# A fused two-layer backbone on one core: how the first stage normalises, turns and empties its token tiles

## The chip, the cores and the metric

The kernel runs on one core of a Trainium2 chip. Its engines are named as the profile names them: PE is TensorE (matrix products, and transposes as products with an identity matrix), DVE is VectorE, ACT is ScalarE, POOL is GpSimd, SP is SyncE, which here only issues DMA transfers. The metric is the time of one execution on the device in microseconds (us); the trace comes from one profiled execution.

## The reference

Two consecutive layers work on 512 latent tokens and 256 context tokens of 1024 features. The first layer mixes tokens by gated linear attention and softmax attention, the second by a gated recurrence, and each ends with a SwiGLU block. Every sub-layer begins with an RMS norm and a shift and scale computed from a conditioning vector. Only the first of these matters here:

```python
def _rms(x, gain, eps=1e-6):
    y = xf * lax.rsqrt(jnp.mean(xf * xf, axis=-1, keepdims=True) + eps)
    ...
m_lat = jnp.split((sc @ mod_w[l] + mod_b[l])[:, None, :], 6, axis=-1)
h_lat = _modulate(_rms(x_lat, norm_pre_mix[l]), m_lat[0], m_lat[1])   # h * (1 + scale) + shift
... h @ w_in ...
```

## The kernel before

Tokens are handled in six tiles of 128: tiles 4 and 5 hold the context, 0 to 3 the latents, and the first stage takes them in the order 4, 5, 0, 1, 2, 3. A tile arrives with tokens on the 128 partitions. Products need the features there, so a tile is first normalised, then turned by TensorE in eight 128 x 128 transposes into an accumulator of 1024 columns (`mm_tile`, of which there are two), and then copied into `xT`. Matrix products use a number split in a high and a low part, and three products for one.

`turn(t)` does this for one tile. `sumsq` has ScalarE square the tile and sum each row, then read out the sum (`ss`). `rstd` (lines 684 and 686) divides by the length and adds the epsilon on VectorE (`ms`), and raises to the power -1/2 on POOL (`rs`). VectorE scales the tile in place (line 1945). After the transposes ScalarE empties the first half of the accumulator and VectorE the second (line 1952). `issue_after` only puts VectorE's scaling of a tile behind an earlier instruction in VectorE's queue: here behind VectorE's copy of the tile two places earlier.

`warm(n)` issues n products of the identity with itself into an unused accumulator `idle`. Each is two matmul rows in the trace. `sums(qd, ks)` multiplies the conditioning vectors with one quarter of the modulation weights `mraw`, `cols(qd)` turns the result into columns (`modrows`, `modT`, `modcol`, `aff`), and `apply` computes scale and shift of two feature blocks of `xT` twice: on ScalarE rounded into the high part (line 2005), and on VectorE in full (line 2006), from which the high part is subtracted (line 2007). `z(t0, qd)` multiplies with a quarter of the first projection (`nat`), whose raw numbers `zraw` are split by `weights(qd)`: the high part on ScalarE (line 792), the low part `wL` on POOL (line 793). The loads of `mraw` and `zraw` are issued by SP, 16 pairs and four pieces; nine buffers hold the pairs, so the tenth pair and later ones wait until `sums` has used an earlier one.

The order on each engine is set by a scheduler that models the time of each instruction. Between `self.pinned = True` and `False` TensorE's instructions stay in the order in which they are written; the other queues are ordered by the model, so an edit can move instructions that it does not name. `self.behind()` puts what follows behind the instructions in `self.latest` in their queues.

Of the kernel before, what the change touches and what calls it, by code (L numbers as in the profile page):

```python
# [8 lines left out]
F32 = mybir.dt.float32  # L9
F32R = mybir.dt.float32r  # L10
BF16 = mybir.dt.bfloat16
U8 = mybir.dt.uint8
AF = mybir.ActivationFunctionType
ALU = mybir.AluOpType
# [3 lines left out]
P = 128  # L18
D = 1024
KD = D // P  # L20
# [7 lines left out]
EPS = 1e-6  # L28
# [288 lines left out]
class Net:  # L317
# [371 lines left out]
    def sumsq(self, src, junk=None, ss=None):  # L689
        if junk is None:  # L690
            junk = self.wp.tile([P, D], BF16, tag="mraw", bufs=2, name="junk")[:, : src.shape[-1]]
        if ss is None:
            ss = self.sm.tile([P, 1], F32, tag="ss", name="ss")
        self.squared = self.nc.scalar.activation(junk, src, AF.Square, accum_out=ss)
        return ss

    def pre_norm(self, pool, t, xt, A, B, h, xn):

        nc = self.nc
        r = 0 if t < LT else 1  # L700
        forms = isinstance(h, Forms)
        if forms:
            xn = pool.tile([P, D], F32, tag="xn", bufs=2, name=f"xn{t}")
        rs = self.rstd(self.sumsq(xt, xn if forms else None), D)
        yield
        if not forms:
            self.mark = nc.vector.tensor_scalar(xn, xt, rs, None, op0=ALU.mult)
            self.pair.append(xn)
            if len(self.pair) == 2:
                self.turns.append(self.pair_turn(pool, t - 1, self.pair, A, B, h))  # L710
                self.pair = []
            return
        self.mark = nc.vector.tensor_scalar(xn, xt, rs, None, op0=ALU.mult)

        def turn():
            for hf in range(2):
                pt = self.tr_tile(f"hT{t}{hf}")
                f = h.at(hf, t)
                for kk in range(4):
                    k = hf * 4 + kk  # L720
                    self.tr(pt[:, kk * P : (kk + 1) * P], xn[:, k * P : (k + 1) * P], self.ident)
                for kk in range(4):
                    k = hf * 4 + kk
                    src = pt[:, kk * P : (kk + 1) * P]
                    nc.scalar.activation(f[:, kk, :], src, AF.Identity, bias=B[:, r, k : k + 1], scale=A[:, r, k : k + 1])
                h.put(hf, t)

        self.turns.append(turn)
# [375 lines left out]
    def even_mixer(self, h, mix, z):  # L1104
# [141 lines left out]

        self.pinned = True
        run("qk0 e m qk0 e e v0 qk0 e e m qk0 e e m v0 e e m m q v0 m m v0 m m kv q m q m q m m m m m m m m m m qk1 kv m")
        tp.release()
        gp = self.open_pool("gla")  # L1250
        run("c0 l0 kv m c0 kv c0 v1 qk1 c0 p p qk1 c0 l0 p qk1 l0 c0 g0 qk1 l0 p c1 p v1 l0 p v1 l0 c1 p v1 l0 c1 l1 g1 g0 c1 g0 r0 c1 l1 r0 g0 l1")
        self.tc.keep_in_program_order(nc.scalar.preload_act_table_set("exp_and_others"))
        run("r0 c1 g1 x l1 x g1 l1 x x l1 x l1 x")
        gp.release()
        mg.__exit__(None, None, None)
# [652 lines left out]
    def run(self):  # L1908
        nc, I, out = self.nc, self.I, self.out
# [13 lines left out]
        order = (4, 5, 0, 1, 2, 3)  # L1923
# [4 lines left out]
        with self.pool("pre0") as pp:  # L1928
            xT = pp.tile([P, KD, NT], F32, name="xT")
# [7 lines left out]
            emptied = []  # L1937

            def turn(t):
                xt = xts.pop(t)  # L1940
                ss = self.sumsq(xt)
                with ExitStack() as behind:
                    if len(emptied) > 1:
                        behind.enter_context(self.tc.issue_after(emptied[-2][1].ins))
                    nc.vector.tensor_scalar(xt, xt, self.rstd(ss, D), None, op0=ALU.mult)
                pt = self.mm_tile(f"xT{t}")
                for k in range(KD):
                    self.tr(pt[:, k * P : (k + 1) * P], xt[:, k * P : (k + 1) * P], self.ident)
                for hf in range(2):
                    dst = xT[:, hf * 4 : hf * 4 + 4, t * P : (t + 1) * P]  # L1950
                    src = pt[:, 512 * hf : 512 * hf + 512].rearrange("p (k i) -> p k i", k=4)
                    self.latest = [*self.latest[-1:], (nc.vector.tensor_copy if hf else nc.scalar.copy)(dst, src)]
                emptied.append(self.latest)

            self.mod_tiles(0, (0, 1))
            A = self.cst.tile([P, 2, 8], F32, name="aff01")
# [4 lines left out]
            def loads(qd):  # L1961
                for k in range(0, KD, 2):
                    u = pp.tile([P, 2, 2, 256], F32, tag="mraw", bufs=9, name=f"mraw00{qd}{k}")
                    for kk in range(2):
                        nc.sync.dma_start(
                            out=u[:, kk],
                            in_=I["mod_w"][0, (k + kk) * P : (k + kk + 1) * P, 0:2048].rearrange("p (m f) -> p m f", m=2)[
                                :, :, 256 * qd : 256 * qd + 256
                            ],
                        )  # L1970
                    us[qd, k] = u
                src = w[256 * qd : 256 * qd + 256, 1536 : 1536 + 288].rearrange("(k p) m -> p k m", p=P)
                zu.append(self.fetched(src, 2, 288, pp.tile([P, 576], F32, tag="zraw", bufs=4, name="zraw")))

            def sums(qd, ks):
                if ks[0] == 0:
                    accs[qd] = (self.sc_tile("mod_acc", qd) if qd < 2 else self.tr_tile("mod_acc"))[:, :P]
                for k in ks:
                    for j in range(4):
                        self.mm(  # L1980
                            accs[qd][32 * j : 32 * j + 32, :],
                            self.scT[:, k, :],
                            us[qd, k // 2 * 2][:, k % 2, j // 2, (j % 2) * P : (j % 2) * P + P],
                            start=(k == 0),
                            stop=(k == KD - 1),
                            tile_position=(0, 32 * j),
                        )
                if ks[-1] == KD - 1:
                    accs[qd] = self.mod_cols(0, accs[qd], P, [(m, r, 2 * qd, 2 * m, r, 2) for m in range(2) for r in range(2)])
# [9 lines left out]
            def apply(qd, r, t0, n):  # L1999
                tok = slice(t0 * P, (t0 + n) * P)  # L2000
                for k in range(2 * qd, 2 * qd + 2):
                    H, L = h.hl(k, tok)
                    a, b = A[:, r, k : k + 1], B[:, r, k : k + 1]
                    f = pp.tile([P, SEQ], F32, tag="xa", bufs=4, name="xa")[:, : n * P]
                    cast = nc.scalar.activation(H, xT[:, k, tok], AF.Identity, bias=b, scale=a)  # L2005
                    nc.vector.tensor_scalar(f, xT[:, k, tok], a, b, op0=ALU.mult, op1=ALU.add)
                    self.mark = nc.vector.tensor_tensor(L, f, H.bitcast(F32), op=ALU.subtract)
                    self.latest = cast, self.mark

            def weights(qd):  # L2010
                with self.behind():
                    zu[qd] = zu[qd](vector=nc.gpsimd)
# [20 lines left out]
            fetch(*order)  # L2033
            for qd in range(4):
                loads(qd)
            for t, n in zip(order[:-1], (1, 2, 2, 3, 3)):
                turn(t)
                self.warm(n)
            sums(0, lo)
            turn(order[-1])  # L2040
            self.warm(3)
            sums(0, hi)
            weights(0)
            self.warm(2)
            cols(0)
            self.warm(5)
            apply(0, 1, 4, 2)
            apply(0, 0, 0, 4)
            for qd in range(1, 4):
                z(4, qd - 1)  # L2050
                sums(qd, lo)
                z(0, qd - 1, (0,))
                sums(qd, hi)
                weights(qd)
                z(0, qd - 1, (1,))
                cols(qd)
                z(2, qd - 1)
                apply(qd, 1, 4, 2)
                apply(qd, 0, 0, 4)
# [217 lines left out]
```

## Time and profile before

| What | Value |
|---|---|
| Device time, median of 3 runs | 1681.68 us (1681.31 to 1683.89) |
| Profiled execution, its own time | 1683.77 us |
| Its span, first to last instruction | 1681.9 us |
| TensorE busy | 1647.9 us, 98% |
| VectorE busy | 1311.9 us, 78% |
| ScalarE busy | 915.6 us, 54% |
| POOL busy | 127.4 us, 8% |
| Mean granted TensorE clock | 0.998 of full speed |

A row of the timeline gives start, duration, engine, line, operation, output and inputs, shapes, and how many instructions were merged; in brackets stands how long the engine was idle before it and what released it. A row of the windows gives, for a stretch of time, the busy time of PE, PEld (the weight loads beside the products), DVE, ACT and POOL with their instruction counts, then the granted clock, the share of the DMA engines and their GB/s. A row of groups gives a line, its forms and count, the busy time and the mean duration in ns.

### The profile page before, as it was taken

How to read it: one execution, taken by the hardware profiler on the slowest of the kernel's cores; microseconds unless marked ns; L12 is line 12 of the kernel's file. 1: busy time of each engine (PE TensorE's matmuls, PEld its weight loads, DVE VectorE, ACT ScalarE, POOL GpSimd, SP SyncE). 2: the span in 40 equal slices, each digit the busy share in tenths (PEclk: the TensorE clock that was granted, in tenths of full speed). 3: DMA queues.
4: the chain of work that ended last, by engine and by line, in shares of the span. 5: the costliest groups of instructions: out<-in, count | busy, mean ns of one | idle time of the engine just before them, and what ended most of it. 6: DMA issues, size and time to landing. Idle time of an engine off the chain costs nothing.

```text
span 1681.9 us, 32570 instructions
## 1 busy us (share of the span) xinstructions
PE 1647.9 (98%) x13425; PEld 1484.2 (88%) x13425; DVE 1311.9 (78%) x2106; ACT 915.6 (54%) x1554; POOL 127.4 (8%) x133
## 2 busy tenths in 40 slices
PE   8999998999999999999999999999999999999998
PEld 7899987888999999998887788888888899999886
DVE  4889768876898988768668648788775589988887
ACT  4645557846544443445447536566564565555564
POOL 2004200001000000002101000000000100000310
PEclk9999999999999999999999999999999999999999
DMA  9651002164253446249515542121125333433973
GB/s 332 190 155 42 2 27 101 52 199 156 85 150 101 141 144 189 79 134 223 100 57 210 191 132 64 52 60 43 52 62 152 125 103 114 123 101 101 221 167 138
DMA packets 184736, 204.79 MB, mean 122 GB/s; under 512 B 7142, under 2 KB 141836, under 8 KB 184588
## 3 DMA queue, kind: packets, MB, share of 16 engines
q1 hardware_dynamic: 173996, 181.98, 34.6%
q0 software_dynamic: 9024, 17.30, 5.9%
q10 hardware_dynamic: 1568, 3.43, 0.6%
q8 instruction: 105, 1.72, 0.4%
q14 instruction: 43, 0.35, 0.1%
HBM read 193.23 MB, written 9.46 MB: 121 GB/s over the span
## 4 chain that ended last, share of the span: by engine, by line
PE 83%; DVE 9%; DMA 3%; ACT 3%; issue 2%; POOL 0%; DVEq 0%; SPq 0%; ACTq 0%; POOLq 0%
PE nat L355 12%; PE a L355 10%; PE ff L355 8%; PE E L355 7%; PE x L355 7%; PE oproj L355 6%; PE o L355 5%; PE b L355 3%; PE D L355 3%; PE fq L355 3%; PE gqk L355 2%; PE pearly L355 2%; PE q L355 2%; PE S L355 2%; PE poh L355 1%
## 5 line engine op out<-in xcount | busy, mean ns | idle before, releaser
L355 PE MATMUL nat<-wH,x 128*128 128x256 f32 (+2 forms) x968 | 226.7, 322 | 0.8 <-ACT x L2005 0.2
L849 ACT CAST wH<-raw 128x1024 fp32r<-128x1024 f32 x120 | 124.8, 1050 | 105.1 <-DVE raw L874 40.1
L355 PEld LDWEIGHTS nat<-wH,x 128*128 128x128 f32 x968 | 162.0, 190 | 19.1 <-ACT natq L1185 1.7
L850 DVE TENSOR_TENSOR wL<-raw,wH 128x1024 fp32r<-128x1024 f32 x120 | 145.6, 1220 | 25.1 <-ACT wH L849 24.5
L355 PE MATMUL nat<-wL,x 128*128 128x256 f32 (+2 forms) x484 | 153.5, 317 | 1.8 <-DVE wL L793 1.8
L793 DVE TENSOR_TENSOR wL<-raw,wH 128x1024 fp32r<-128x1024 f32 x79 | 95.7, 1221 | 48.5 <-ACT wH L792 47.7
L355 PE MATMUL ff<-x,wH 128*128 128x512 f32 (+1 forms) x512 | 127.7, 340 | 0.0
L686 POOL TENSOR_TENSOR rs<-ms,neghalf 128x1 f32<-128x1 f32 (+2 forms) x62 | 62.9, 1018 | 793.9 <-DVE ms L684 793.8
L792 ACT CAST wH<-raw 128x1024 fp32r<-128x1024 f32 x79 | 82.2, 1050 | 66.9 <-PE ff L355 20.0
L355 PE MATMUL oproj<-wH,x 128*128 128x512 f32 x320 | 102.2, 394 | 0.4 <-ACT x L1319 0.4
L355 PEld LDWEIGHTS nat<-wL,x 128*128 128x128 f32 x484 | 92.1, 190 | 7.8 <-DVE wL L793 2.6
L615 DVE SCALAR_TENSOR_TENSOR macc<-mraw,scT,macc 128x1024 f32<-128x1024 f32 x70 | 88.0, 1279 | 11.5 <-DMA mraw<-in_mod_w_dram 11.3
L355 PEld LDWEIGHTS ff<-x,wH 128*128 128x128 f32 x512 | 87.3, 190 | 10.0
L355 PE MATMUL x<-wH,two 128*128 128x512 f32 x280 | 90.5, 392 | 0.8 <-DVE y L1840 0.7
L1762 POOL DMA_DIRECT2D t<-in_ffn_w_down_dram x36 | 41.8, 1199 | 642.5 <-DVE t L1801 335.0
L1001 ACT COPY qkh<-arr 128x512 f32<-128x512 f32 x112 | 70.0, 641 | 36.4 <-DVE arr L1006 32.2
L355 PE MATMUL ff<-x,wL 128*128 128x256 f32 (+1 forms) x256 | 86.2, 337 | 0.0
L874 DVE TENSOR_TENSOR raw<-raw 128x512 f32<-128x512 f32 x120 | 82.7, 689 | 2.8
L1006 DVE TENSOR_TENSOR arr<-arr,f 128x512 f32<-128x512 f32 x112 | 74.1, 686 | 1.9 <-ACT qkh L1001 0.3
L355 PE MATMUL a<-T,wH 128*128 128x384 f32 (+1 forms) x320 | 70.6, 309 | 2.0 <-ACT qb L912 1.2
L355 PEld LDWEIGHTS oproj<-wH,x 128*128 128x128 f32 x320 | 59.9, 188 | 13.1 <-ACT x L1319 1.0
L355 PE MATMUL a<-x,dH 128*128 128x384 f32 (+1 forms) x320 | 70.4, 309 | 1.0 <-ACT go L922 0.6
(423 smaller groups left out, 4558.7 us busy)
## 6 DMA issues: line engine op xcount, KB each, us to landing
mraw<-in_mod_w_dram SPq DMA_DIRECT2D x80, 512.0 KB, 4.2
raw<-in_ffn_w_gate_dram SPq DMA_DIRECT2D x44, 512.0 KB, 3.9
raw<-in_ffn_w_up_dram SPq DMA_DIRECT2D x44, 512.0 KB, 4.8
raw<-in_odd_w_in_dram SPq DMA_DIRECT2D x40, 512.0 KB, 3.8
t<-in_ffn_w_down_dram POOLq DMA_DIRECT2D x30, 512.0 KB, 8.5
raw<-in_ffn_w_down_dram SPq DMA_DIRECT2D x28, 512.0 KB, 7.7
mraw<-in_mod_w_dram SPq DMA_DIRECT2D x32, 256.0 KB, 6.2
raw<-in_even_w_in_dram SPq DMA_DIRECT2D x16, 512.0 KB, 5.9
```

The source lines that it names most:

```text
L355: return self.pin(self.nc.tensor.matmul(*a, **k))
L615: nc.vector.scalar_tensor_tensor(a, u, w, a, op0=ALU.mult, op1=ALU.add)
L686: nc.gpsimd.tensor_tensor(rs, ms, self.neghalf.to_broadcast([P, w]), op=ALU.pow)
L792: self.casts = self.casts[-1:] + [nc.scalar.copy(H[:, :m], raw[:, :m])]
L793: vector.tensor_tensor(L[:, :m], raw[:, :m], H[:, :m].bitcast(F32), op=ALU.subtract)
L849: self.nc.scalar.copy(H, f)
L850: self.nc.vector.tensor_tensor(L, f, H.bitcast(F32), op=ALU.subtract)
L874: add = lambda o, x, y: nc.vector.tensor_tensor(o, x, y, op=ALU.add)
L1001: nc.scalar.copy(qkv[:, :, :, half, :], dst)
L1006: nc.vector.tensor_tensor(dst, dst, tb, op=ALU.mult)
L1762: add = lambda o, src: self.pin(nc.gpsimd.dma_start(out=o, in_=src, accum_op=ALU.add))
```

## The change

Five edits, all in the first stage. `mean_rstd` replaces `sumsq` and `rstd` for these six tiles: ScalarE's square gets the factor 1/32, so that its sum is the mean already, and POOL adds the epsilon and takes the power; VectorE has no part. An accumulator is emptied by one engine in one copy of 1024 columns: VectorE takes the first, second and fifth tile in order (4, 5 and 2), ScalarE the others (0, 1 and 3). The scaling of the third tile is no longer put behind a copy; that of the fourth stands behind the first tile's copy, those of the fifth and sixth behind the second's. Behind tile 5's transposes 18 identity products follow in place of 2. `self.latest` is set by hand for `weights(0)`, which it puts behind the last two copies. The new name in `apply` changes no instruction.

```diff
+    def mean_rstd(self, src):
+        nc = self.nc
+        junk = self.wp.tile([P, D], BF16, tag="mraw", bufs=2, name="junk")
+        ms = self.sm.tile([P, 1], F32, tag="ss", name="ss")
+        self.squared = nc.scalar.activation(junk, src, AF.Square, scale=1.0 / 32, accum_out=ms)
+        rs = self.sm.tile([P, 1], F32, tag="rs1", name="rs")
+        nc.gpsimd.tensor_scalar(ms, ms, EPS, None, op0=ALU.add)
+        nc.gpsimd.tensor_tensor(rs, ms, self.neghalf, op=ALU.pow)
+        return rs
...
             def turn(t):
                 xt = xts.pop(t)
-                ss = self.sumsq(xt)
+                rs = self.mean_rstd(xt)
                 with ExitStack() as behind:
-                    if len(emptied) > 1:
-                        behind.enter_context(self.tc.issue_after(emptied[-2][1].ins))
-                    nc.vector.tensor_scalar(xt, xt, self.rstd(ss, D), None, op0=ALU.mult)
+                    if len(emptied) > 2:
+                        behind.enter_context(self.tc.issue_after(emptied[min(len(emptied) - 3, 1)].ins))
+                    nc.vector.tensor_scalar(xt, xt, rs, None, op0=ALU.mult)
...
-                for hf in range(2):
-                    dst = xT[:, hf * 4 : hf * 4 + 4, t * P : (t + 1) * P]
-                    src = pt[:, 512 * hf : 512 * hf + 512].rearrange("p (k i) -> p k i", k=4)
-                    self.latest = [*self.latest[-1:], (nc.vector.tensor_copy if hf else nc.scalar.copy)(dst, src)]
-                emptied.append(self.latest)
+                copy = nc.vector.tensor_copy if len(emptied) in (0, 1, 4) else nc.scalar.copy
+                emptied.append(copy(xT[:, :, t * P : (t + 1) * P], pt.rearrange("p (k i) -> p k i", k=KD)))
...
-            for t, n in zip(order[:-1], (1, 2, 2, 3, 3)):
+            for t, n in zip(order[:-1], (1, 18, 2, 3, 3)):
                 turn(t)
                 self.warm(n)
             sums(0, lo)
             turn(order[-1])
             self.warm(3)
             sums(0, hi)
+            self.latest = emptied[5], emptied[4]
             weights(0)
```

VectorE's queue at the program's start, before. `xt4` is tile 4 as loaded, `xT4` its accumulator, `xT_122` the turned tokens; numbers behind an underscore tell buffers apart.

```order
L684 TENSOR_SCALAR ms_197<-ss_195 128x1
L684 TENSOR_SCALAR ms_217<-ss_215 128x1
L1945 TENSOR_SCALAR xt4_126<-xt4_126,rs_199 128x1024
L1945 TENSOR_SCALAR xt5_128<-xt5_128,rs_219 128x1024
L419 COPY col_103<-pt_rows_109 128x128
L1952 COPY xT_122<-xT4_202 128x4x128
L684 TENSOR_SCALAR ms_238<-ss_236 128x1
L1945 TENSOR_SCALAR xt0_130<-xt0_130,rs_240 128x1024
L1952 COPY xT_122<-xT5_222 128x4x128
L684 TENSOR_SCALAR ms_259<-ss_257 128x1
L1945 TENSOR_SCALAR xt1_132<-xt1_132,rs_261 128x1024
```

The same queue now.

```order
L1956 TENSOR_SCALAR xt4_126<-xt4_126,rs_197 128x1024
L1956 TENSOR_SCALAR xt5_128<-xt5_128,rs_215 128x1024
L1956 TENSOR_SCALAR xt0_130<-xt0_130,rs_250 128x1024
L419 COPY col_103<-pt_rows_109 128x128
L1961 COPY xT_122<-xT4_201 128x8x128
L1961 COPY xT_122<-xT5_219 128x8x128
L1956 TENSOR_SCALAR xt1_132<-xt1_132,rs_269 128x1024
L1956 TENSOR_SCALAR xt2_134<-xt2_134,rs_289 128x1024
L1956 TENSOR_SCALAR xt3_136<-xt3_136,rs_326 128x1024
L1961 COPY xT_122<-xT2_293 128x8x128
```

The scaling of tile 0 now stands ahead of the copies of tiles 4 and 5, the scalings of tiles 1 to 3 right behind those, and the six means are gone.

TensorE's queue at the same place, as a difference. `idle` rows are the identity products, `xT` rows the turns of tiles 4, 5, 0 and 1.

```order
-L358 MATMUL xT_222<-ident,xt_128 128x128 x8
+L358 MATMUL xT_219<-ident,xt_128 128x128 x8
+L355 MATMUL idle<-ident 128x128 x18
+L358 MATMUL xT_254<-ident,xt_130 128x128 x8
 L355 MATMUL idle<-ident 128x128 x2
-L358 MATMUL xT_243<-ident,xt_130 128x128 x8
-L355 MATMUL idle<-ident 128x128 x2
-L358 MATMUL xT_264<-ident,xt_132 128x128 x8
+L358 MATMUL xT_273<-ident,xt_132 128x128 x8
```

The turn of tile 0 (`xt_130`) now follows 18 identity products; everything behind it keeps its order.

POOL's queue now. Before, six powers (line 686) stood here alone.

```order
L704 TENSOR_SCALAR ss_195<-ss_195 128x1
L704 TENSOR_SCALAR ss_213<-ss_213 128x1
L705 TENSOR_TENSOR rs_197<-ss_195,neghalf_99 128x1
L705 TENSOR_TENSOR rs_215<-ss_213,neghalf_99 128x1
L704 TENSOR_SCALAR ss_248<-ss_248 128x1
L705 TENSOR_TENSOR rs_250<-ss_248,neghalf_99 128x1
```

The model puts the addition of tile 5 ahead of the power of tile 4. On ScalarE three whole copies (tiles 0, 1 and 3) stand where six halves stood, and on SP the last piece of `zraw` moves from behind the last quarter's `mraw` loads to behind the first two of these eight.

More of the change, by code (lines that the diff above doesn't have):

```diff
@@ L2003, in apply @@
                     a, b = A[:, r, k : k + 1], B[:, r, k : k + 1]
+                    x = xT[:, k, tok]
                     f = pp.tile([P, SEQ], F32, tag="xa", bufs=4, name="xa")[:, : n * P]
-                    cast = nc.scalar.activation(H, xT[:, k, tok], AF.Identity, bias=b, scale=a)
-                    nc.vector.tensor_scalar(f, xT[:, k, tok], a, b, op0=ALU.mult, op1=ALU.add)
+                    cast = nc.scalar.activation(H, x, AF.Identity, bias=b, scale=a)
+                    nc.vector.tensor_scalar(f, x, a, b, op0=ALU.mult, op1=ALU.add)
                     self.mark = nc.vector.tensor_tensor(L, f, H.bitcast(F32), op=ALU.subtract)
```

## The prediction

> **What bounds it now.** The page's engine table comes first: TensorE is busy 98% of the span, so a microsecond taken out of its queue anywhere is worth about a microsecond, and one taken from another engine is worth what TensorE waits for it.
>
> ```profile
> PE 1647.9 (98%) x13425; PEld 1484.2 (88%) x13425; DVE 1311.9 (78%) x2106; ACT 915.6 (54%) x1554; POOL 127.4 (8%) x133
> ```
>
> The change lies in the first 28 us, so I then read the timeline there. I call a 128-token tile by its number: 4 and 5 are context, 0 to 3 latent, taken in the order 4, 5, 0, 1, 2, 3.
>
> ```profile
> 1.64 5.99 PE L355 MATMUL idle<-ident 128*128 128x128 f32 x36 [1.64 <-POOL ident masks.py:199]
> ...
> 6.79 0.19 ACT L694 ACTIVATION_READ_ACCUMULATOR junk<-xt 128x1 f32 x1
> ...
> 7.10 0.75 DVE L1945 TENSOR_SCALAR xt<-xt,rs 128x1024 f32<-128x1024 f32 x1
> 7.25 1.02 POOL L686 TENSOR_TENSOR rs<-ms,neghalf 128x1 f32<-128x1 f32 x1 [0.72 <-DVE ms L684]
> ...
> 7.95 1.05 PE L358 MATMUL xT<-ident,xt 128*128 128x128 f32 x8
> ...
> 8.30 0.75 DVE L1945 TENSOR_SCALAR xt<-xt,rs 128x1024 f32<-128x1024 f32 x1 [0.45 <-POOL rs L686]
> ...
> 9.11 1.09 PE L358 MATMUL xT<-ident,xt 128*128 128x128 f32 x8
> ...
> 12.39 1.05 ACT L1952 COPY xT<-xT 128x512 f32<-128x512 f32 x2
> ...
> 12.98 0.69 DVE L1952 COPY xT<-xT 128x512 f32<-128x512 f32 x1 [3.73 <-ACT xT L1952]
> ...
> 13.81 0.55 POOL L686 TENSOR_TENSOR rs<-ms,neghalf 128x1 f32<-128x1 f32 x1 [5.55 <-DVE ms L684]
> 14.40 0.75 DVE L1945 TENSOR_SCALAR xt<-xt,rs 128x1024 f32<-128x1024 f32 x1 [0.66 <-POOL rs L686]
> ...
> 15.30 1.78 PE L358 MATMUL xT<-ident,xt 128*128 128x128 f32 x8 [4.65 <-DVE xt L1945]
> ```
>
> TensorE turns tiles 4 and 5 by 10.2 and then waits 4.65 us for tile 0 to be scaled. VectorE had not begun that: its next instruction was its half of emptying tile 4's accumulator, which waited 3.73 us for ScalarE's half, and ScalarE had all six squares ahead of it until 12.39. The windows show a second price.
>
> ```profile
> 8.62:10.65 2.03, 2.03 (x18) 1.76 (x16) 0.63 (x2) 1.88 (x3) 0.00 (x0) 1.00 1.01 394
> 10.65:15.30 4.65, 0.00 (x1) 0.03 (x1) 1.65 (x4) 2.62 (x7) 0.55 (x1) 1.00 1.10 350
> ...
> 15.45:18.87 3.42, 3.42 (x18) 3.42 (x18) 1.87 (x5) 0.59 (x1) 0.79 (x2) 0.51 1.10 358
> ```
>
> The column ahead of the last two is the granted clock. After the empty 4.65 us it is 0.51 for 3.42 us and then full again; the last but one is the share of the DMA engines, at 1.0 and over. The chain of waits gives what TensorE does from there to tile 3, the last tile turned.
>
> ```profile
> 15.30 1.78 PE xT L358 x8
> 17.08 0.85 PE idle L355 x4
> 17.93 1.41 PE xT L358 x8
> 19.34 0.67 PE idle L355 x6
> 20.01 0.10 issue
> ...
> 21.85 1.01 PE mod_acc L355 x32
> 22.86 1.02 PE xT L358 x8
> ```
>
> So 7.56 us from tile 0 to tile 3, and from tile 3 the rest of the stage follows TensorE's own queue until the first product of the projection.
>
> ```profile
> 16.48 0.75 DVE L1945 TENSOR_SCALAR xt<-xt,rs 128x1024 f32<-128x1024 f32 x1 [0.66 <-POOL rs L686]
> ...
> 17.11 0.59 ACT L1952 COPY xT<-xT 128x512 f32<-128x512 f32 x1 [3.67 <-PE xT L358]
> ...
> 17.73 0.69 DVE L1952 COPY xT<-xT 128x512 f32<-128x512 f32 x1 [0.50 <-ACT xT L1952]
> ...
> 19.21 0.75 DVE L1945 TENSOR_SCALAR xt<-xt,rs 128x1024 f32<-128x1024 f32 x1 [0.73 <-POOL rs L686]
> ...
> 25.15 1.41 POOL L793 TENSOR_TENSOR wL<-zraw,wH 128x576 fp32r<-128x576 f32 x1 [3.71 <-ACT wH L792]
> ...
> 27.65 0.40 PE L355 MATMUL nat<-wH,x 128*128 128x288 f32 x1 [0.23 <-ACT x L2005]
> ...
> 27.89 0.29 PE L355 MATMUL nat<-wL,x 128*128 128x288 f32 x1
> ```
>
> **Norms on POOL.** Six VectorE instructions at line 684 go, and six additions on POOL come. No row shows a POOL addition of one column; the nearest are these, with two copies of the new width further down the list.
>
> ```profile
> masks.py:199 POOL TENSOR_SCALAR_AFFINE_SELECT ident<-ident 128x128 f32<-128x128 f32 x1 | 0.3, 288 | 0.0
> ...
> L386 POOL MEMSET neghalf<- 128x1 f32 x1 | 0.1, 97 | 0.0
> ...
> L764 DVE TENSOR_TENSOR pn<-oproj,gv 128x1024 f32<-128x1024 f32 x10 | 12.2, 1220 | 16.3 <-ACT junk L694 16.1
> ...
> L694 ACT ACTIVATE junk<-oproj 128x1024 bf16<-128x1024 f32 x10 | 10.2, 1019 | 25.4 <-PE oproj L355 25.4
> ```
>
> I take 0.29 us, since the select is also a one-input operation with constants, with 0.10 (the memset) and 0.55 (the power) as ends. POOL's queue now holds addition 4, addition 5, power 4, power 5, so power 4 still waits for the second square, read out at 6.98. POOL starts about 0.09 after what it waits for (the second mean ended at 7.16, the power began at 7.25). Addition 5 runs 7.07 to 7.36 and power 4 ends at 7.91. Scaling 4 starts 0.03 later (8.27 to 8.30 above), runs 7.94 to 8.69, and the turn of tile 4 starts 0.10 after that (7.85 to 7.95), at 8.79 where it was at 7.95. Power 5 overlaps scaling 4. In the row at 7.25 such a power took 1.02 and ended 0.42 after the scaling beside it; so it ends at 9.11, and scaling 5 at 9.89. The turn of tile 4, 1.02 by the chain's row, ends at 9.81, its one identity product (two matmul rows of 0.112) at 10.03, so tile 5 is turned from 10.03 to 11.05.
>
> The Trainium skill, "SBUF — State Buffer", section "Who interferes with whom", has it that whichever of the two issues first keeps the shared ports for its whole instruction and the other blocks. The row at 7.25 agrees, the scaling having begun first; here power 5 would issue at 7.91, ahead of the scaling at 7.94, and by that rule scaling 4 would lose 0.55, the turn of tile 5 would end at 11.60, and the gain below would be 1.38 in place of 1.93.
>
> **Scalings ahead of copies, one engine for an accumulator.** VectorE no longer meets the wait of 3.73 us: scaling 0 stands ahead of the copies. Its addition and power need 0.84 of POOL after 9.11, or end 0.42 past scaling 5 at 10.3 if they are held, so it ends by about 11.1, and the copies of tiles 4 and 5 follow whole, 1.22 each by the row with a 1024-wide accumulator operand, after one of 128 columns: by 12.6 and 13.8. Scalings 1 to 3 of 0.75 are done by 16.1. ScalarE's whole copies take 1.02 against 0.59 for a half. Both lie beside TensorE's identity products. What is late next is neither of them.
>
> **Sixteen more identity products.** TensorE must finish 18 of them, 36 rows at 0.112 us (0.67 for six in the chain), 4.02 us, before it may turn tile 0: 11.05 to 15.07. Tile 0 and its accumulator are ready at about 12.6, so the products are the bound, and the turn begins only 0.23 earlier than 15.30. But TensorE is not empty for 4.65 us any more; I expect no stretch at 0.5. Then four turns' worth of queue costs, at full speed, 3 turns of 1.02, four identity rows 0.45, twice six at 0.67 and the sums 1.01: 5.86 in place of 7.56. Tile 1 wants its scaling (by 14.6) and tile 5's accumulator (13.8) at 16.5; tile 2 wants ScalarE's copy of tile 0 (about 17.2) at 18.2. All come in time. Tile 3 starts at 15.07 + 5.86 = 20.93 instead of 22.86.
>
> **Sum.** 0.23 from the earlier turn and 1.70 from the clock: 1.93 us against the profiled execution's 1683.77 (span 1681.9 and 1.87 around it), which would be 1681.84. The square's new factor and the renamed operand of the affine step issue the same instructions as before, and POOL's next work is not due until 25.15: nothing for these. Behind tile 3 nothing changes but that ScalarE's last copy is 0.43 longer, so the low weights come 0.43 later against tile 3; they ended at 26.56 and were wanted at 27.89, which covers it, and without that cover it would cost what exceeds 1.33. The profiled execution is 2.1 above the median of 1681.68, and I can't say how the unprofiled runs fell on the clock. Had the clock stayed full there, tile 0 would have been turned 0.7 sooner, but VectorE would then bind: it is free for the copy of tile 0 only when scaling 1 ends at 17.23, and copy, mean and power ahead of scaling 2 take 1.48 (17.73 to 19.21): scaling 2 done at 19.46, turn at 19.56 for 20.11, only 0.55 better. So the gain against such runs is 1.38. I take the middle, 1.65: 1681.68 - 1.65 = 1680.0.
>
> Ends: with the addition at 0.10 and power 5 not held, tile 5's turn ends at 10.86 and the gain is 2.12. With 0.55 and scaling 4 held, it ends at 11.86: 1.12, less 0.55 for an undisturbed clock, 0.57.
>
> **The loads.** The third and fourth quarter's loads on SP's queue wait for buffers that the sums free, and one load of the projection's weights is moved ahead of six of the last quarter's. Both matter only if the DMA engines, full at this time, come late.
>
> ```profile
> L355 PE MATMUL mod_acc<-mraw,scT x256: 272/273/297, 21.8 to 48.6; 128*32 128x128 f32 x128
> L1965 SPq DMA_DIRECT2D mraw<-in_mod_w_dram x32: 367/368/1092, 5.8 to 33.9; - x32
> ...
> DMA to landing us min/median/max: 4.6/6.2/7.4
> ```
>
> The last load is issued at 33.9 and lands by 41.3; its product is at 48.6, about 47 after the change. A load of 128 x 2 x 288 numbers, 0.295 MB, moved ahead at 350 GB/s (last column of the windows) costs it 0.84. That leaves some 5 us, so I count no loss.
>
> **Rivals.** First, POOL costs more than I think, as at the high end: gain 0.6 to 1.1, some 1680.8. For it, that powers of one column take longer elsewhere:
>
> ```profile
> 366.35 1.53 POOL L686 TENSOR_TENSOR rs<-ms,neghalf 128x1 f32<-128x1 f32 x1 [63.58 <-DVE ms L684]
> ```
>
> Second, the slow side: POOL's queue, addition 5 and both powers at 1.53 each. Power 4 then ends at 10.13, scaling 4 at 10.9, power 5 at 11.66, scaling 5 at 12.44, and tile 5's turn at 13.6. TensorE would stand empty from 7.8 to 11, lose the clock as it did after 10.65 (another 1.70), and the 36 rows would end at 17.6 or later: 0.6 + 1.7 slower, 1684.0. The change loses time once tile 5's turn ends after 12.98 (22.86 less 5.86 and 4.02). Against it: the power at 13.81 took 0.55, and nothing on VectorE but two scalings overlaps these.
>
> Third, the clock falls all the same between the turn of tile 5 and tile 0. The identity rows would run at 0.213 (0.85 for four in the chain) from about 12 to 15.45: 9 rows before, 16 in the slow stretch, 11 after, ending at 16.7, tile 3 at 22.5, gain 0.3: 1681.4. Against it: 8.62 to 10.65 is mostly turns, and the clock stayed 1.00 through it. The Trainium skill, "TensorE: Matmul & The Clock Gate", "Part 4: PE-mode transpose", says that transposes do not count as busy time in the same way; no row here shows that they fail to hold the clock, and by that rule this third case is what would happen.
>
> Fourth, the change does nothing: TensorE's earlier start is spent waiting for `mraw`, 1681.7. Against it the 5 us above.
>
> **Numbers.** Forecast 0.68; POOL dearer 0.14; slow side 0.08; clock falls 0.05; transfers 0.05. The range holds the ends (1679.6 to 1681.1), the third and fourth case, and something for the shown runs' spread of 1681.31 to 1683.89: 1678.4 to 1682.2. A difference of 0.2%, 3.4 us, is about what a measurement of this kernel can tell. No case gains that much; only the best end, 2.12, with a median 1.2 lower by chance gives it: 0.08 for faster. Slower by as much needs the slow case well beyond its 2.3: 0.05. The rest, 0.87, is within it.
>
> **What would show it.** Right: tile 4 turned near 8.8; tile 0 near 15.1, following the identity products with no gap; granted clock 1.00 from 10 to 20; tile 3 near 20.9, the first projection product near 25.7; no wait of TensorE on `mraw` before 50. Wrong: an addition far from 0.3, an empty TensorE ahead of tile 4 of over 3 us, a slow clock within 9 to 21, or a TensorE wait on VectorE's copies.

## The result and the profile after

| What | Before | After |
|---|---|---|
| Device time, median of 20 runs each | 1681.74 us (1679.95 to 1684.77) | 1679.93 us (1678.06 to 1681.13) |
| Ratio after/before | | 0.9985, 95% interval 0.9978 to 0.9991 |
| Profiled execution, its own time | 1683.77 us | 1680.16 us |
| Its span | 1681.9 us | 1678.4 us |
| First product of the projection | 27.65 us | 25.22 us |

The whole run is 0.15% shorter by the ratio, 1.5 to 3.7 us by its interval. The middle lies under the 0.2% (3.4 us) that was taken for what a measurement of this kernel can tell, the upper end a little above. The stage itself can be read far more finely, because both traces begin alike. The timeline after, the same stretch as was shown of before:

```profile
7.35 1.39 POOL L705 TENSOR_TENSOR rs<-ss,neghalf 128x1 f32<-128x1 f32 x2
...
7.95 1.58 DVE L1956 TENSOR_SCALAR xt<-xt,rs 128x1024 f32<-128x1024 f32 x2 [7.95 <-POOL rs L705]
...
8.76 1.09 PE L358 MATMUL xT<-ident,xt 128*128 128x128 f32 x8 [0.59 <-DVE xt L1956]
8.83 0.78 POOL L704 TENSOR_SCALAR ss<-ss 128x1 f32<-128x1 f32 x1
...
9.91 1.04 PE L358 MATMUL xT<-ident,xt 128*128 128x128 f32 x8
...
10.29 0.75 DVE L1956 TENSOR_SCALAR xt<-xt,rs 128x1024 f32<-128x1024 f32 x1 [0.76 <-POOL rs L705]
...
10.79 4.18 PE L355 MATMUL idle<-ident 128*128 128x128 f32 x36
...
11.16 2.35 DVE L1961 COPY xT<-xT 128x1024 f32<-128x1024 f32 x2
...
11.86 0.22 POOL L704 TENSOR_SCALAR ss<-ss 128x1 f32<-128x1 f32 x1
...
14.81 1.04 PE L358 MATMUL xT<-ident,xt 128*128 128x128 f32 x8
...
20.32 1.09 PE L358 MATMUL xT<-ident,xt 128*128 128x128 f32 x8
...
23.11 1.41 POOL L804 TENSOR_TENSOR wL<-zraw,wH 128x576 fp32r<-128x576 f32 x1 [8.90 <-ACT wH L803]
...
24.27 0.26 DVE L2003 SCALAR_TENSOR_TENSOR aff<-modcol,col 128x4 f32<-128x4 f32 x1
...
25.22 0.40 PE L355 MATMUL nat<-wH,x 128*128 128x288 f32 x1 [0.26 <-ACT x L2014]
```

Tile 4 is turned at 8.76 and tile 5 at 9.91, 0.8 later than before; the 36 identity rows follow at once and tile 0 behind them at 14.81 with no idle time in brackets. VectorE no longer waits for ScalarE: scaling 0 begins at 10.29, the two whole copies at 11.16. The chain of waits of the same run gives TensorE's queue (start, duration, what):

```profile
10.95 4.02 PE idle L355 x36
14.97 0.87 PE xT L358 x8
15.84 0.45 PE idle L355 x4
16.29 0.87 PE xT L358 x8
...
19.38 1.01 PE mod_acc L355 x32
20.39 1.02 PE xT L358 x8
```

And the windows (busy times of PE, PEld, DVE, ACT, POOL, then the granted clock, DMA share and GB/s) have no slow stretch, where before 15.45 to 18.87 had 0.51:

```profile
10.65:14.81 4.16, 4.16 (x40) 4.16 (x39) 4.16 (x7) 1.70 (x5) 3.14 (x6) 1.00 1.10 350
14.81:20.32 5.51, 5.51 (x75) 5.19 (x73) 1.91 (x3) 2.03 (x2) 0.00 (x0) 1.00 1.10 356
```

TensorE's waits of the first 75 us are these alone (us in total, times, longest); none is for `mraw` and none for a copy:

```profile
PE idle L355 <- POOL ident masks.py:199: 1.6, 1, 1.6
PE xT L358 <- DVE xt L1956: 0.6, 1, 0.6
PE nat L355 <- ACT x L2014: 0.3, 1, 0.3
```

So the stage gains 2.43 us at the first product. The spans differ by 3.5. Set beside each other instruction by instruction, the changed kernel leads by 2.4 up to 160 us, by 1.0 from 208 to 600, and by about 2.0 from 680. The fall stands at two places in its profile, 161.78 and 206.27 us, where TensorE had been idle for 0.56 and 0.46 us and nothing is shown that it waited for. Near 1373 us the lead jumps by about 2, where the profiled run of before had this row among TensorE's waits from 1360 to 1430:

```profile
PE a L355 <- ACT qb L912: 1.2, 1, 1.2
```

With two smaller waits beside it, it lost 2.1 us. A second profiled execution of the kernel before, told below, has no TensorE wait in that stretch, and one of the experiments has them again, so this part comes and goes by itself.

### The profile page after: what moved, and what is told of

The parts are those of the page before. It is cut to its first block, busy times and chain, and to the rows that moved or that the text cites. A ratio compares the mean times of both kernels' runs of the same rounds, so it can differ in the third digit from the quotient of the medians.

```text
span 1678.4 us, 32622 instructions
## 1 busy us (share of the span) xinstructions
PE 1649.9 (98%) x13457; PEld 1486.4 (89%) x13457; DVE 1311.4 (78%) x2097; ACT 915.6 (55%) x1551; POOL 131.5 (8%) x139
## 4 chain that ended last, share of the span: by engine, by line
PE 83%; DVE 8%; ACT 3%; DMA 3%; issue 2%; POOL 0%; DVEq 0%; SPq 0%; ACTq 0%; POOLq 0%
PE nat L355 12%; PE a L355 10%; PE ff L355 8%; PE E L355 7%; PE oproj L355 6%; PE x L355 6%; PE o L355 4%; PE D L355 4%; PE b L355 4%; PE fq L355 3%; PE gqk L355 2%; PE pearly L355 2%; PE q L355 2%; PE S L355 2%; PE poh L355 1%
## 5 line engine op out<-in xcount | busy, mean ns | idle before, releaser
L355 PE MATMUL E<-T,wH 128*128 128x384 f32 (+1 forms) x320 | 70.4, 309 | 0.6 <-DVE go L938 0.6
```

Of the source, the lines that this page charges most:

```text
L355: return self.pin(self.nc.tensor.matmul(*a, **k))
```

## Experiments

The theory: TensorE's order after tile 5 is limited by what empties the accumulators; one engine for an accumulator removes the wait of one engine for another, and the 18 identity products then cost more than the clock that they keep. The rivals: the products pay, since the clock falls without them; or the gain is the early scaling, or the mean on POOL. "Lead" is the start of the first projection product, 27.65 in the profile before, less that of the run named.

**Two products in place of 18**, all else as changed.

```diff
-            for t, n in zip(order[:-1], (1, 18, 2, 3, 3)):
+            for t, n in zip(order[:-1], (1, 2, 2, 3, 3)):
```

> The changed kernel with 2 identity products behind tile 5, as before the change, in place of 18. Theory A (the products only keep TensorE's clock up, and at 18 they are themselves what tile 0 waits for): tile 0 is turned when VectorE has emptied tile 4's accumulator, near 12.4 us in place of 14.8; tile 1 when it is scaled, near 14.3; tile 3 near 18.4 in place of 20.3; the first projection product near 23.2 in place of 25.2; TensorE is empty for only about 1 us, so the granted clock stays at 1.00; whole time 2 us below the changed kernel, 1678. Rival B (without them the clock falls to half after tile 5, as in the kernel before, because turns do not hold it up): a stretch of 3.4 us at 0.5 between 11 and 19, tile 3 near 20, and little or no gain on the changed kernel.

Its timeline:

```profile
12.55 1.09 PE L358 MATMUL xT<-ident,xt 128*128 128x128 f32 x8 [1.06 <-DVE xT L1961]
...
14.43 1.06 PE L358 MATMUL xT<-ident,xt 128*128 128x128 f32 x8 [0.34 <-DVE xt L1956]
...
23.55 0.40 PE L355 MATMUL nat<-wH,x 128*128 128x288 f32 x1 [0.26 <-ACT x L2014]
```

1677.52 us, ratio 0.9971 (0.9962 to 0.9981). Tile 0 now waits 1.06 us for VectorE to empty tile 4's accumulator and is still 2.26 earlier; the granted clock stays 1.00 from 11.49 to 18.65. The lead is 4.10, so in the changed kernel the sixteen added products cost 1.67 us at the first product and bought nothing. They may cost more later: such idle times of TensorE between 160 and 210 us stand in all three traces with 18 products (the changed kernel and the next two experiments) and in none of the eight with two, and here the lead of 4.10 is still 4.05 at 240 us. Why, no run shows.

**The 18 products alone**, in the kernel before.

```diff
-            for t, n in zip(order[:-1], (1, 2, 2, 3, 3)):
+            for t, n in zip(order[:-1], (1, 18, 2, 3, 3)):
```

> The kernel before with 18 identity products behind tile 5 and nothing else of the change. Theory A (keeping the clock is worth only 0.55 us to the old order, because VectorE's and POOL's work between two tiles binds as soon as TensorE is fast): tile 0 still turned at 15.3 or a little later, tile 3 near 22.3 in place of 22.8, first projection product near 27.1. Rival B (the change's gain is the clock): tile 3 near 21.1, first projection product near 25.9. On the whole time: if the runs of the kernel before near 1683.8 are those in which the clock fell, this kernel has none of them; A says its times lie about 0.5 under the slow group and no more than that, so that the two groups must come from elsewhere.

```profile
15.41 1.07 PE L358 MATMUL xT<-ident,xt 128*128 128x128 f32 x8 [0.62 <-DVE xt L1945]
...
26.26 0.16 DVE L1995 SCALAR_TENSOR_TENSOR aff<-modcol,col 128x4 f32<-128x4 f32 x1
...
27.17 0.40 PE L355 MATMUL nat<-wH,x 128*128 128x288 f32 x1 [0.23 <-ACT x L2005]
```

1681.85 us, ratio 0.9996 (0.9988 to 1.0005). The products do keep the clock, and that was worth 0.48 us to the old order: once TensorE runs at full speed, it waits for VectorE's scalings, 1.6 us in three waits. One of its 11 runs still took 1683.82 us, so the longer times are not the clock's fall alone.

**The mean on VectorE again**, all else as changed.

```diff
-                rs = self.mean_rstd(xt)
+                rs = self.rstd(self.sumsq(xt), D)
```

> The changed kernel with the mean on VectorE again (line 684) and everything else of the change. Theory A (moving the mean gains nothing): tile 4 is turned at 8.0 in place of 8.8, and tile 5 ends near 10.1, so the identity products end near 14.1; but the six means stand ahead of VectorE's copies, the last waits for the sixth square at 12.4, and tile 1 starts near 16.0, tile 3 near 20.1, first projection product near 25.0, within 0.3 of the changed kernel's 25.2. Rival B (VectorE's means were a cost on the path): first product 0.6 or more later, 25.8 or over.

```profile
7.95 1.07 PE L358 MATMUL xT<-ident,xt 128*128 128x128 f32 x8
...
12.74 2.35 DVE L1961 COPY xT<-xT 128x1024 f32<-128x1024 f32 x2
...
25.02 0.40 PE L355 MATMUL nat<-wH,x 128*128 128x288 f32 x1 [0.26 <-ACT x L2014]
```

One profiled execution, 1679.8 us. Tile 4 is turned 0.81 earlier, as before the change, the copies start 1.58 later behind the six means, and the first product comes 0.20 earlier. The mean on POOL gains nothing here, where the 18 products cover it.

**Accumulators emptied in halves again**, with two products.

```diff
-                copy = nc.vector.tensor_copy if len(emptied) in (0, 1, 4) else nc.scalar.copy
-                emptied.append(copy(xT[:, :, t * P : (t + 1) * P], pt.rearrange("p (k i) -> p k i", k=KD)))
+                for hf in range(2):
+                    ...
+                    self.latest = [*self.latest[-1:], (nc.vector.tensor_copy if hf else nc.scalar.copy)(dst, src)]
+                emptied.append(self.latest[1])
...
-            self.latest = emptied[5], emptied[4]
```

> The kernel with 2 identity products behind tile 5, and each accumulator emptied in two halves again, the first on ScalarE, the second on VectorE. With 18 products this would be hidden, so it is tried where nothing covers it. Theory A (an accumulator shared by both engines waits for ScalarE's six squares): VectorE's half of tile 4 begins near 13.0 us, behind ScalarE's; tile 0 is turned near 13.8 in place of 12.55, tile 1 near 15.2 in place of 14.4, tile 3 near 19.5 in place of 18.65, first projection product near 24.4 in place of 23.55. Rival B (only the order of the scalings mattered): tile 0 within 0.2 of 12.55 and the first product within 0.2 of 23.55.

Timeline and windows:

```profile
10.39 0.76 DVE L1956 TENSOR_SCALAR xt<-xt,rs 128x1024 f32<-128x1024 f32 x1 [0.72 <-POOL rs L705]
...
12.99 0.69 DVE L1963 COPY xT<-xT 128x512 f32<-128x512 f32 x1 [1.65 <-ACT xT L1963]
...
13.74 1.10 PE L358 MATMUL xT<-ident,xt 128*128 128x128 f32 x8 [2.23 <-DVE xT L1963]
...
25.82 0.40 PE L355 MATMUL nat<-wH,x 128*128 128x288 f32 x1 [0.23 <-ACT x L2017]
```

```profile
14.68:18.09 3.41, 3.41 (x19) 3.41 (x18) 2.21 (x5) 1.17 (x2) 0.00 (x0) 0.50 1.10 358
```

One profiled execution, 1679.35 us. VectorE's half again waits for ScalarE's (1.65 us), TensorE stands empty for 2.23, and the clock is lost for 3.41. Tile 0 came as expected, the first product not: 25.82 and not 24.4, since neither theory had reckoned with the clock. One engine for an accumulator is worth 25.82 less 23.55, 2.27 us, beside the other edits: 1.19 at tile 0, and 1.08 behind it, where the slow stretch lies. The run shows a second thing. With halves it still leads the kernel before by 27.65 less 25.82, 1.83 us, from the mean on POOL and the earlier scalings alone. In both, VectorE's half of tile 4 begins at 12.98 or 12.99; but here scaling 0 was over at 11.15, and tile 0 is turned as soon as the accumulator is free, at 13.74, where before its mean, power and scaling followed the half and it was turned at 15.30. That is 1.56 of the 1.83.

**Scaling 0 behind VectorE's copies**, with two products.

```diff
-                    if len(emptied) > 2:
-                        behind.enter_context(self.tc.issue_after(emptied[min(len(emptied) - 3, 1)].ins))
+                    if len(emptied) > 1:
+                        behind.enter_context(self.tc.issue_after(emptied[max(0, min(len(emptied) - 3, 1))].ins))
```

> The kernel with 2 identity products behind tile 5, and the scaling of tile 0 put behind VectorE's copies of tiles 4 and 5 again; accumulators still emptied by one engine. Theory A (VectorE's work up to tile 1 is the same sum in either order, and tile 1 needs all of it): tile 0 turned near 13.15 us, 0.6 later than without this edit, but tile 1 near 14.5 and the first projection product near 23.6, within 0.15 of 23.55. Rival B (the scaling ahead of the copies is the gain): everything 0.6 later, first product near 24.15.

```profile
13.11 1.06 PE L358 MATMUL xT<-ident,xt 128*128 128x128 f32 x8 [1.66 <-DVE xt L1956]
...
14.46 1.04 PE L358 MATMUL xT<-ident,xt 128*128 128x128 f32 x8
...
23.55 0.40 PE L355 MATMUL nat<-wH,x 128*128 128x288 f32 x1 [0.25 <-ACT x L2014]
```

```profile
13.11:18.10 4.99, 4.99 (x57) 4.87 (x61) 2.96 (x4) 2.03 (x2) 1.20 (x1) 1.00 1.10 355
```

One profiled execution, 1680.85 us. Tile 0 is 0.56 later, tile 1 hardly, and the first product is at 23.55, exactly where it is with the early scaling. So where one engine empties an accumulator, the scaling ahead of the copies gives nothing either. (The whole run is longer than with two products alone by what came later: its lead drops from 4.94 near 750 us to 3.22 by 790, and TensorE waits 1.8 us between 1360 and 1430, as in the profiled run of before.)

**Each addition on POOL behind the power of the tile ahead**, with two products, so that tile 4's power no longer waits for tile 5's square.

```diff
+        with ExitStack() as behind:
+            if self.power is not None:
+                behind.enter_context(self.tc.issue_after(self.power.ins))
+            nc.gpsimd.tensor_scalar(ms, ms, EPS, None, op0=ALU.add)
-        nc.gpsimd.tensor_scalar(ms, ms, EPS, None, op0=ALU.add)
-        nc.gpsimd.tensor_tensor(rs, ms, self.neghalf, op=ALU.pow)
+        self.power = nc.gpsimd.tensor_tensor(rs, ms, self.neghalf, op=ALU.pow)
```

> The changed kernel with 2 identity products behind tile 5, and each addition on POOL put behind the power of the tile before, so that the power of tile 4 no longer waits for the square of tile 5. Theory A (first stage is now a chain of norms, scalings and VectorE's copies): power 4 ends near 6.6 in place of 7.9, tile 4 turned near 8.0, tile 5 near 9.1, tile 0 near 11.6, tile 1 near 13.5, tile 3 near 17.6, first projection product near 22.5; 0.7 us below the kernel with 2 products alone, about 1677.3. Rival B (the loads bind as soon as TensorE is this early): TensorE waits for mraw ahead of the sums near 17 or 19, and the first product stays near 23.2.

```profile
11.73 1.09 PE L359 MATMUL xT<-ident,xt 128*128 128x128 f32 x8 [0.71 <-DVE xT L1965]
...
22.73 0.40 PE L356 MATMUL nat<-wH,x 128*128 128x288 f32 x1 [0.26 <-ACT x L2018]
```

1676.43 us, ratio 0.9966 (0.9954 to 0.9979), lead 4.92: 0.82 more than with two products alone, where 0.7 was expected. TensorE waits for no `mraw`.

**The same without the identity products behind tiles 0 to 3.**

```diff
-            for t, n in zip(order[:-1], (1, 2, 2, 3, 3)):
+            for t, n in zip(order[:-1], (1, 2, 0, 0, 0)):
...
             turn(order[-1])
-            self.warm(3)
```

> The kernel with additions and powers by tiles on POOL and 2 identity products behind tile 5, now with no identity products between tiles 0, 1, 2 and 3 and behind tile 3. Theory A (they are bare cost on TensorE's queue here, and turns hold the clock up): tile 1 near 13.6 as before this edit, tile 2 near 14.5, tile 3 near 16.4, granted clock 1.00 throughout, first projection product 20.5 to 21.0 in place of 22.73, since the last of the eight loads of the first quarter lands near 17.3 to 18.3 and the sums then wait for it by up to 1 us; whole time 1.7 to 2.2 lower, about 1674.5. Rival B (turns do not count as busy time): between 10.9 and 15.4 TensorE has turns alone, the clock falls to 0.5 within 9 to 19 for 3.4 us, and the first product comes near 22 or later. Rival C (the loads give all of it back further on): TensorE waits for mraw in the third or fourth quarter and the lead has shrunk by 1 us or more at 60 us.

Timeline and windows:

```profile
11.78 1.09 PE L359 MATMUL xT<-ident,xt 128*128 128x128 f32 x8 [0.93 <-DVE xT L1965]
...
19.33 1.41 POOL L808 TENSOR_TENSOR wL<-zraw,wH 128x576 fp32r<-128x576 f32 x1 [5.78 <-ACT wH L807]
...
19.82 0.93 DVE L2007 SCALAR_TENSOR_TENSOR aff<-modcol,col 128x4 f32<-128x4 f32 x1
...
21.44 0.40 PE L356 MATMUL nat<-wH,x 128*128 128x288 f32 x1 [0.93 <-ACT x L2018]
```

```profile
11.78:15.53 3.75, 2.96 (x25) 2.59 (x25) 3.06 (x4) 2.46 (x5) 1.34 (x3) 1.00 1.10 348
15.53:18.95 3.42, 3.42 (x76) 2.86 (x76) 1.47 (x2) 1.53 (x3) 0.00 (x0) 1.00 1.10 360
```

1675.72 us, ratio 0.9962 (0.9949 to 0.9976), lead 6.21. From 11.78 to 15.53 TensorE does three turns with gaps and nothing else, and the clock is 1.00 there and after. TensorE waits for no `mraw`, yet the first product came at least 0.44 later than the expectation, and the whole run is some 0.7 below the version before it in place of 1.7 to 2.2. The rows say why the first product was late: `aff`, a step on four columns, took 0.93 and ended at 20.75, with POOL's `wL` (20.74).

**The split of the weights earlier**, behind ScalarE's copy of tile 1 and not of tile 3, to move `wL` off `aff`.

```diff
-            self.latest = emptied[5], emptied[4]
+            self.latest = emptied[3], emptied[4]
```

> The version without identity products behind tile 0 and later, with the split of the first projection weights put behind ScalarE's copy of tile 1 in place of that of tile 3. In the version before it the affine step aff (four columns, two inputs from the on-chip memory) took 0.93 us, 19.82 to 20.75, and ended with POOL's low weights wL (19.33 to 20.74), and the first projection product came at 21.44. Theory A, aff is held by wL for as long as that runs: the high part wH now waits for its load (issued at 11.86, 5.9 to landing: about 17.8) and runs to 18.5, wL from 18.55 to 19.95, so aff, still due at 19.82, takes 0.16 to 0.3 and the first product comes at 20.7 to 20.9. Theory B, aff is slow for another reason (the full DMA engines, its own operands): it takes about 0.9 wherever wL stands, first product at 21.4. By either the whole run moves by 0.7 us at most, less than it can tell: 1675.0 to 1675.8. If the load lands later than 18.2, ScalarE's copy of tile 3 waits behind wH, and the first product of tile 3 with it, which is not due before 23.

```profile
18.73 0.67 ACT L807 CAST wH<-zraw 128x576 fp32r<-128x576 f32 x1 [2.34 <-DMA zraw<-in_even_w_in_dram]
...
19.48 1.41 POOL L808 TENSOR_TENSOR wL<-zraw,wH 128x576 fp32r<-128x576 f32 x1 [4.65 <-ACT wH L807]
...
20.44 0.47 DVE L2007 SCALAR_TENSOR_TENSOR aff<-modcol,col 128x4 f32<-128x4 f32 x1
...
21.59 0.40 PE L356 MATMUL nat<-wH,x 128*128 128x288 f32 x1 [0.47 <-ACT x L2018]
```

1675.70 us, ratio 0.9956 (0.9943 to 0.997): not to be told from the version before it. The load landed 0.9 later than estimated, so `wL` could not start before 19.48; tile 3 was turned 0.62 later in this run, and the first product came 0.15 later, not at 20.7 to 20.9. But `aff` again ends (20.91) where `wL` ends (20.89), now after 0.47 and not 0.93. Where `wL` is over when it starts, as in the run with 18 products alone, it takes 0.16. So `aff` ends with `wL` whenever it begins during it; what is left of the hold is now the load's.

**The kernel before, once more.**

> The kernel before, unchanged, for one more trace. Its times fall in two groups near 1681.5 and 1683.7. Theory A (whether the clock falls depends on where the free-running window lies in TensorE's empty 4.65 us; the groups come from elsewhere): where the clock does not fall, the first projection product is near 27.2 in place of 27.65, which is a quarter of the distance of the groups. Rival B (the groups are the clock's fall): a trace without the fall has a span near 1679.8, one with it near 1681.9, and the difference stands at the first product already.

Windows, and the first product:

```profile
13.68:20.51 6.83, 5.13 (x24) 5.16 (x25) 3.81 (x9) 1.17 (x2) 1.65 (x3) 0.50 1.10 353
```

```profile
28.26 0.40 PE L355 MATMUL nat<-wH,x 128*128 128x288 f32 x1 [0.23 <-ACT x L2005]
```

1682.07 us. Here the clock was lost for 6.83 us, twice the stretch of the first profile, and the first product came 0.61 later than in it. The span is 1680.2 us all the same, 1.7 shorter than the first profile's: rival B does not hold.

How the stage's lead and the whole run agree, where several executions were timed (the gain is the interval of the ratio on 1682 us):

| Version | Lead at the first product, us | Gain of the whole run, us |
|---|---|---|
| The change | 2.43 | 1.5 to 3.7 |
| 18 products alone | 0.48 | -0.8 to 2.0 |
| Two products | 4.10 | 3.2 to 6.4 |
| Two products, additions in turn | 4.92 | 3.5 to 7.7 |
| No products behind tile 0 | 6.21 | 4.0 to 8.6 |
| Weights earlier | 6.06 | 5.0 to 9.6 |

Each lead lies within its interval, and would also if it were counted from the second profile of before (0.61 more each). The intervals are 2 to 5 us wide, so this agrees with a run that gains what its stage gains and does not prove it.

## Why the prediction came out as it did

The order of events was right. The sum, 1.93, was 0.50 smaller than the stage's gain, and that the forecast time came within 0.1 us of the median is in part luck.

- **Norms on POOL.** Tile 4 at 8.79 was right (8.76). The addition took 0.21 to 0.23 alone, not 0.29; two of the six stood beside a scaling and took 0.78, which was named as a sign of being wrong and cost nothing, since the products were the bound. Power 5 did not run 0.42 past the scaling: the two powers end at 7.35 + 1.39 = 8.74, just behind scaling 4, so both scalings were done at 9.53 and not at 9.89. It made no difference, since tile 5 follows tile 4's turn on TensorE.
- **The rule on ports.** By the sentence cited from the Trainium skill, "SBUF — State Buffer", section "Who interferes with whom", scaling 4 would have lost 0.55 to power 5. The two scalings took 1.58 together, twice the usual 0.75 and a little, though the powers ran from 7.35 to 8.74: VectorE was not held. What stretched was POOL's side, the two powers to 1.39 in place of twice 0.57, and the additions beside scalings to 0.78.
- **The products as the bound.** Right, and its price stood in the working: tile 0 was said to be ready at about 12.6, and with two products it was turned at 12.55.
- **Turns behind tile 0: the mis-sized term.** It was 5.86, with 1.02 for each of three turns. The chain has 5.42 (14.97 to 20.39): each of the three follows identity products and takes 0.87 there; 1.02 stands only at tile 3, which follows the sums. That is 0.44 of the 0.50 by which 1.93 fell short of 2.43. Another 0.10 came ahead of it: the products ended at 14.97 and not at 15.07, mostly because tile 5's turn follows a product too and took 0.87. Behind tile 3 the stage then took 0.04 more than before.
- **The clock.** No slow stretch came, as expected. Its worth to the old order was estimated at 0.55 and is 0.48.
- **The middle of two gains.** 1.65 was taken between 1.38 and 1.93. The profiles give 1.95 against an undisturbed clock (27.17 less 25.22), 2.43 against one stretch and 3.04 against two. The medians differ by 1.81, less than any of these, with an interval of 1.5 to 3.7. So 1680.0 came near to 1679.93 by luck: the stage gained more than the working said, and the run gave part of it back, perhaps at the idle times between 160 and 210 us, which the working did not have.
- **Cover behind tile 3.** `wL` ends at 24.52 and was wanted at 25.46: covered, as said. That it holds `aff` was not seen; in the changed kernel that cost 0.10 (0.26 for 0.16). It was no more with two products (0.25 or 0.26), and 0.93 once there were none behind tile 0.
- **Loads.** No wait on `mraw`, also in the versions that are four to six us earlier.
- **Rivals.** POOL dearer and the slow side fell at tile 4's 8.76. The clock fell in no run of the changed kernel. By the rule cited from the Trainium skill, "TensorE: Matmul & The Clock Gate", "Part 4: PE-mode transpose", turns would not have held it; the windows of the version without products behind tile 0 show that they do, at 1.00 through three turns with gaps.

The runs add up in steps from the kernel before to the changed one. The mean on POOL and the earlier scalings, with accumulators still emptied in halves, bring the first product from 27.65 to 25.82, 1.83 gained; which of the two does it was not tried. One engine for an accumulator brings it to 23.55, 2.27 more. The sixteen products put it back to 25.22, 1.67 lost, which leaves 2.43. What an edit is worth depends on the others: with one engine for an accumulator, the early scaling (tried with two products) and the mean on POOL (tried with the 18 products) are each within 0.2 of nothing.

## What to carry to other kernels

An accumulator emptied by two engines is free only when the later of the two queues gets to it; give each to one engine and take them by turns. Products that keep the clock belong into a gap that stays open: count what the gap will be after the other edits, since a turn that could have started stands behind them. An edit that is worth nothing beside the others may be worth much without them, so take edits out one at a time and also add up the steps. And price an instruction by the row with the same neighbours: a turn behind identity products was 0.87 in the chain, one behind the sums 1.02.

## What the runs showed of the hardware

- The clock was kept through an empty TensorE of 1.66 us (scaling 0 behind the copies) and lost after 2.23 us (halves). The stretch lost was 3.42 and 3.41 us in two runs and 6.83 in a second run of the kernel before. The clock changes at a fixed step: in the profile before at 15.49, at 18.90 and, TensorE's work being over, at 1677.78, which is 486 times 3.413 later. Counted back from the last change of each trace, these are the steps that held the two gaps, the first with halves, the second with scaling 0 behind the copies (the first busy time is TensorE's):

```profile
11.27:14.68 3.41, 1.18 (x12) 0.99 (x11) 1.76 (x4) 2.17 (x5) 2.14 (x5) 1.00 1.10 348
10.57:13.98 3.41, 1.75 (x16) 1.59 (x15) 3.41 (x5) 1.87 (x5) 2.75 (x6) 1.00 1.10 351
```

The two losses of the kernel before followed steps with 0.18 and 0.72 us of work, and in the second run the next step, with 1.71 at the slow clock, did not bring it back. Over all eleven traces from end to end, every step at full clock with 1.43 us of work or less was followed by a slow one, and none with 1.66 or more. So in these runs the work within a step decides, and not the gap alone: the same gap costs one step or two by where the steps' edges fall in it. In the version without products behind tile 0 the step from 11.89 to 15.30 holds 2.62 us of turns and nothing else, and the clock stayed at 1.00. In the 38 runs of the kernel before that were timed beside the experiments the mean granted clock was never above 0.998; in the 20 of the changed kernel never under 0.998.
- A one-column addition on POOL took 0.21 to 0.23 us alone and 0.78 beside a scaling on VectorE, ending just after it; the scaling kept its 0.75.
- The other way round, VectorE's `aff`, which reads two inputs from the on-chip memory, ended 0.01 to 0.02 us after POOL's `wL` whenever it began during it, after 0.25 to 0.26, 0.47 or 0.93 us. The Trainium skill, "SBUF — State Buffer", section "Who interferes with whom", says that a VectorE instruction with two such inputs contends with a POOL instruction that reads there; these rows agree.
- The kernel before took 1679.95 to 1685.2 us. In its first 20 runs no time lies between 1681.9 and 1683.31, which looked like two groups; among the later ones times from 1682.01 to 1682.87 fill that gap. The clock alone does not set them: runs of 1683.49 and 1683.57 had a mean granted clock of 0.998, one of 1680.71 had 0.997. The waits near 1373 us (2.1) could make the difference, but no trace was taken that shows which run had what, so this stays open.
